# The experts' group of 64 + 32 + 32 slots as four column tiles of 32, and third behind the first group

## The chip, the cores and the metric

One core of one Trainium2 chip runs the whole program. The metric is the device time of one execution in microseconds (us). Engines are named as in the profile: PE (TensorE matmul), PEld (its weight load), DVE (VectorE), ACT (ScalarE), POOL (GpSimd), SP (SyncE, which here only issues transfers).

## The reference, cut to what matters

The program is one block of a hybrid model on 256 tokens of width 1024: four mixers, a merge, and then a mixture of 16 experts, all in float32. Only the experts' part is touched:

```
def _hier_moe(h, w_grp, b_grp, w_rt, b_rt, w1, w3, w2):
    ...                                   # group and top 2 experts of each token, combine: 256 x 16
    out = jnp.zeros_like(t)
    for e in range(N_EXPERTS):            # 16 experts, hidden width 512
        y = (jax.nn.silu(t @ w1[e]) * (t @ w3[e])) @ w2[e]
        out = out + combine[:, e:e + 1] * y
    return out.reshape(shp)
```

Each token uses two experts, but every expert has some tokens, so all 16 experts' weights (6.3 MB each) are read.

## The kernel before, in words

**Slots and groups.** Expert 0 has 128 slots of its own. The other 15 experts are ranked on the chip by how many tokens chose them, and a table, `RANK`, gives each rank a group, an offset and a number of slots: three large ranks get 128, 128 and 96, five get 64, seven get 32. A group has 128 slots, one per row of the result, so there are eight groups, which I number 0 to 7 in the order in which they are multiplied:

| Group | before | after | loads (up + down) |
|---|---|---|---|
| 0 | 128 (expert 0) | the same | 8 + 4 |
| 1 | 64 + 64 | the same | 16 + 8 |
| 2 | 128 | the same | 8 + 4 |
| 3 | 128 | **64 + 32 + 32** | 8 + 4, now 24 + 12 |
| 4 | 64 + 64 | **128** | 16 + 8, now 8 + 4 |
| 5 | 64 + 32 + 32 | **64 + 64** | 24 + 12, now 16 + 8 |
| 6 | 32 + 32 + 32 + 32 | the same | 32 + 16 |
| 7 | 96 + 32 | the same | 16 + 10 |

**A group's work.** `gather` fetches the slots' tokens by a matmul with a one-hot matrix (tiles `Dh`, `h2h`, `h2l`), for two groups at once: 1 and 2, 3 and 4, 5 and 6, and 7 alone. `expert_up` multiplies by w1 and w3: eight steps, a step taking one load of 512 KB per expert of the group (two blocks of 128 rows by 512 columns). `hidden` transposes, `expert_down` multiplies by w2 in four steps, and `scatter` adds the rows back to the tokens by a one-hot matmul (tiles `DT`, `yeh`, `yel`). In program order the down part of group g - 1 stands behind the up part of group g.

**Column tiles.** An expert with 32 slots uses 32 of the array's 128 columns, and its result goes to 32 rows of a shared result bank. The helper `subs` says in which pieces an expert's slots are multiplied: before, 96 slots go as three pieces of 32, everything else as one piece. Each float32 matmul of 512 columns stands in the trace as two records (two passes).

**Loads and places.** All weights go through 34 places of 512 KB (tiles wwA, wh, wb, wC, wD, wB and g), handed out in a fixed ring. The first 12 loads (expert 0) come early. The other 180 need the ranking, start at 506.5 us, and all are issued by SP in program order: `wload` (L281 is the line of the helper that records it) takes the next place, and SP waits until the matmuls that last read that place are done. So load n of these 180 can be issued when the place that was released as number n - 22 is free. A step releases its places at its end. The last group's w2 is loaded in narrower cuts, so that the result leaves in pieces.

All instructions carry line L281, that of a recording helper; they are told apart by tiles.

Of the kernel before, what the change touches and what calls it, by code (L numbers as in the profile page):

```python
# [23 lines left out]


NSTAT = 1
RANK = [(1, 0, 128), (2, 0, 128), (6, 0, 96), (0, 0, 64), (0, 64, 64), (3, 0, 64), (3, 64, 64), (4, 0, 64),
        (6, 96, 32), (4, 64, 32), (4, 96, 32), (5, 0, 32), (5, 32, 32), (5, 64, 32), (5, 96, 32)]
NGRP = NSTAT + 1 + max(g for g, _, _ in RANK)
assert len(RANK) == NE - NSTAT  # L30

# [45 lines left out]
def _consts():  # L77
# [14 lines left out]
    def add3(name, a):  # L92
        add(name, a, 2)
# [68 lines left out]
    add3("tie", row(np.where(i4[None, :] < i4[:, None], -1.2e-38, 0.0)))  # L162
    nd = len(RANK)
    add3("rev", row(nd - 1 - np.arange(nd)))
# [3 lines left out]
    add3("scap", row([128] * NSTAT))  # L168
    add3("rbase", row([128 * (NSTAT + g) + o for g, o, n in RANK]))
    add3("rcap", row([n for g, o, n in RANK]))  # L170
    return [np.ascontiguousarray(np.concatenate(o, 1), dtype=np.float32) for o in outs]
# [117 lines left out]
def body(ctx, tc, I, out, dbg=None, upto=None):  # L289
# [55 lines left out]
    def act(o, i, f=AF.Copy, **k):  # L345
        A.activation(out=o, in_=i, func=f, **k)
# [4 lines left out]
    def ts(o, a, s1, s2=None, op0=mul, op1=add, eng=V):  # L351
        if s2 is None:
            eng.tensor_scalar(out=o, in0=a, scalar1=s1, scalar2=None, op0=op0)
        else:
            eng.tensor_scalar(out=o, in0=a, scalar1=s1, scalar2=s2, op0=op0, op1=op1)

    def tt(o, a, b, op=mul, eng=V):
        eng.tensor_tensor(out=o, in0=a, in1=b, op=op)
# [4 lines left out]
    def red(o, i, op=add):  # L363
        return V.tensor_reduce(out=o, in_=i, axis=AX.X, op=op)

    def mmul(o, l, r, start=True, stop=True, shared=False):
        T.matmul(out=o, lhsT=l, rhs=r, start=start, stop=stop, skip_group_check=shared)
# [34 lines left out]
    def tr(o, i):  # L402
        T.transpose(out=o, in_=i, identity=ident[:i.shape[0], :i.shape[0]])
# [505 lines left out]
    for j in range(31):  # L909
        n, w = 31 - j, j + 1  # L910
# [12 lines left out]
    for m in range(32):  # L923
        d, o = m // 16, (m % 16) * 32
# [9 lines left out]
    for m in range(32):  # L934
        d, o = m // 16, (m % 16) * 32
# [20 lines left out]
    for step in range(8):  # L956
# [29 lines left out]
        if step < 7:  # L986
# [5 lines left out]
            for h in range(2):  # L992
                f_ = fch[hv[h], :, :, step:step + 1].to_broadcast([64, 2, 2, 64])
                o = Sn[hv[h], :, :, hv[h]]
# [5 lines left out]
        if step >= 4:  # L1000
            for d, (c8, t_, vs, us, m0, VU) in enumerate(st):
                for i in range(2):
                    o = py[:, i, c8 - 4, :]
# [376 lines left out]
    def sm(name, shape, bufs=1, dt=F32):  # L1380
        return small(name, shape, bufs, p2, dt)
# [32 lines left out]

    nd = len(RANK)
    key = sm("key", [nd])
# [23 lines left out]
    def hb():  # L1440
        return hb_("hb")

    def mb():
        return mb_("mb")
# [86 lines left out]
    def wload(name, e, q):  # L1531

        w = places.pop(0)
        wn[0] += 1
        src = I[name]
        src = src[e] if isinstance(e, int) else src[bass.ds(e, 1)].rearrange("a d n -> (a d) n")
        j = src.shape[0] // 128
        src = src.rearrange("(p j) n -> p j n", j=j)
        jj = j // 4
        if isinstance(q, slice):  # L1540
            ins = SP.dma_start(w[:, :j * (q.stop - q.start)].rearrange("p (j n) -> p j n", j=j), src[:, :, q])
        else:
            ins = SP.dma_start(w.rearrange("p (j n) -> p j n", j=jj), src[:, q * jj:(q + 1) * jj])
        if wn[0] <= MA + 2:
            after(ins, loads[min(wn[0] + 2, len(loads) - 1)])
        return w

    groups = [[(e, 0, 128)] for e in range(NSTAT)] + [[] for _ in range(NGRP - NSTAT)]
# [4 lines left out]
    def eid(e):  # L1553
        if isinstance(e, int):
            return e
        if e not in regs:
            r = e[1]
            regs[e] = nc.values_load(eidi[0:1, r:r + 1], engines=[mybir.EngineType.SP], min_val=0, max_val=NE - 1,
                                     skip_runtime_bounds_check_because="sum over a one-hot of 16 experts")
        return regs[e]  # L1560

    def subs(o, n):
        if n == 96:
            return [(o + k, 32) for k in range(0, 96, 32)]
        return [(o, n)]

    Dw, Dt = (gg[0][:, 0, k * 512:k * 512 + 512].rearrange("p (a s) -> p a s", a=2) for k in range(2))

# [38 lines left out]
    def expert_up(g, between):  # L1607

        k = next(s.index(g) for s in SETS if g in s)
        gs_ = slice(k * 128, k * 128 + 128)  # L1610
        ph = []
        for name in ("w1", "w3"):
            p = hb()
            ph.append(p)
            for q in range(4):
                ws = [wload(name, eid(e), q) for e, _, _ in groups[g]]
                for jj in range(2):
                    j = 2 * q + jj
                    for w, (e, o, n) in zip(ws, groups[g]):
                        for o_, n_ in subs(o, n):  # L1620
                            mmul(p[o_:o_ + n_], gT[:, j, gs_.start + o_:gs_.start + o_ + n_],
                                 w[:, jj * 512:jj * 512 + 512], j == 0, j == 7)
                places.extend(ws)
            if name == "w1":
                between()
        rows = slice(0, max(o + n for _, o, n in groups[g]))
        pd = mb()
        for a in range(2):
            tr(pd[:, a * 128:a * 128 + 128], Dw[:, a, gs_])
        cw_ = sm("cw", [1], 3)  # L1630
        red(cw_, pd[:, :256])
        DT = slots.tile(p2, [P, 256], F32R, "DT", "DT", 3)
        ts(DT, pd[:, :256], 0.0, None, ALU.is_gt)
        a_ = slots.tile(p2, [P, 512], F32, "act", "act", 1)
        act(a_[rows], ph[0][rows], AF.Silu)
        tt(a_[rows], a_[rows], ph[1][rows])
        return a_, rows, cw_, DT
# [10 lines left out]
    def w2s(g):  # L1648
        if g not in down_w:
            down_w[g] = [[wload("w2", eid(e), j) for e, _, _ in groups[g]] for j in range(4)]  # L1650
        return down_w[g]
# [3 lines left out]
    def parts(py, yh, yl, rows, cw_, cs):  # L1655

        t = slots.tile(p2, [P, 512], F32, "sct", "sct", 2)[:, :cs.stop - cs.start]
        tt(t[rows], py[rows], gg[0][rows, 1, cs])
        act(yh[rows, cs], t[rows], AF.Copy, scale=cw_[rows])
        stt(yl[rows, cs], t[rows], cw_[rows], yh[rows, cs].bitcast(F32), mul, sub)  # L1660

    def scatter(yh, yl, rows, DT, cs):

        for a in range(2):
            as_ = slice(a * 128, a * 128 + 128)
            po = mb()[:, :cs.stop - cs.start]
            mmul(po, DT[rows, as_], yh[rows, cs], True, False)
            mmul(po, DT[rows, as_], yl[rows, cs], False, True)
            tt(x2[:, a, cs], po, x2[:, a, cs], add)
# [3 lines left out]
    def expert_down(g, aT, rows, cw_, DT):  # L1673
        yh, yl = (slots.tile(p2, [P, 1024], F32R, n, n, 1) for n in ("yeh", "yel"))
        if g < NGRP - 1:
            py_ = [hb() for _ in range(2)]
            for j in range(4):
                ws = w2s(g)[j]
                for hf in range(2):
                    for w, (e, o, n) in zip(ws, groups[g]):  # L1680
                        for o_, n_ in subs(o, n):
                            mmul(py_[hf][o_:o_ + n_], aT[:, j, o_:o_ + n_], w[:, halves[hf]], j == 0, j == 3)
                places.extend(ws)
            for hf in range(2):
                parts(py_[hf], yh, yl, rows, cw_, halves[hf])
            return yh, yl

        cuts = [0, 256, 512, 768, 896, 1024]
        cols = [slice(a, b) for a, b in zip(cuts, cuts[1:])]
        ws = [[wload("w2", eid(e), cs) for e, _, _ in groups[g]] for cs in cols]  # L1690
        for q in range(len(cols) + 1):
            if q < len(cols):
                py = hb()
                n_c = cols[q].stop - cols[q].start
                for j in range(4):
                    for w, (e, o, n) in zip(ws[q], groups[g]):
                        for o_, n_ in subs(o, n):
                            mmul(py[o_:o_ + n_, :n_c], aT[:, j, o_:o_ + n_], w[:, j * n_c:j * n_c + n_c], j == 0, j == 3)
                places.extend(ws[q])
                parts(py[:, :n_c], yh, yl, rows, cw_, cols[q])  # L1700
            if q:
                cs = cols[q - 1]
                scatter(yh, yl, rows, DT, cs)
                A.dma_start(ov[:, :, cs], x2[:, :, cs])
# [8 lines left out]
    def down(g):  # L1713
        if g >= 0:
            a_, rows, cw_, DT = state[g]["u"]
            state[g]["y"] = expert_down(g, state[g]["aT"], rows, cw_, DT)
# [92 lines left out]
```

## Time and profile before

| | us |
|---|---|
| median of 3 timed runs | 781.92 |
| the three runs | 775.94, 781.92, 784.67 |
| the profiled execution, its own time | 777.15 |
| its span in the trace | 775.4 |

The span is the time from the first to the last recorded instruction; 1.75 us of the execution lie around it. Times in the views count from the span's start. The experts' part is what follows 506 us.

### The profile page before, as it was taken

What the parts mean: (1) busy time and instruction counts of PE and PEld (TensorE: products, weight loads), DVE (VectorE), ACT (ScalarE), POOL (GpSimd) and SP (SyncE); (2) the same over time, 40 slices, a digit from 0 to 9 for tenths busy, and PEclk for the clock granted to TensorE, in tenths of its full rate; (3) what the DMA queues carried; (4) which work ended last, traced back from release to release, by engine and by line L of the source; (5) the groups of instructions that cost most, each with busy time, mean ns of one, the idle gap of its engine ahead of it and who ended that gap; (6) DMA issues with size and microseconds to landing.
All of it is one profiled execution on the core that took longest, in us unless ns stands there. A gap on an engine that the chain in (4) does not pass through costs nothing.

```text
span 775.4 us, 13568 instructions
## 1 busy us (share of the span) xinstructions
PE 716.7 (92%) x5189; PEld 491.1 (63%) x5189; DVE 471.6 (61%) x1002; ACT 277.1 (36%) x524; POOL 83.4 (11%) x85
## 2 busy tenths in 40 slices
PE   2989998998889999999999999889999999999996
PEld 0559986787778676777999997654454451242234
DVE  5586567789994787899996486773241350230214
ACT  4343453344354676743556334511111110010111
POOL 0140011113100110000102280100000000000000
PEclk9999995799987999999999999969999999999999
DMA  8663320123432025567877885089999899879995
GB/s 318 189 251 109 102 89 1 38 86 97 122 97 83 9 76 191 170 196 251 298 280 256 283 299 194 1 302 409 409 409 407 300 398 333 314 288 399 410 390 170
DMA packets 53897, 174.97 MB, mean 226 GB/s; under 512 B 5442, under 2 KB 12482, under 8 KB 53826
## 3 DMA queue, kind: packets, MB, share of 16 engines
q1 hardware_dynamic: 50896, 168.79, 60.4%
q10 hardware_dynamic: 2930, 5.25, 1.9%
q8 instruction: 42, 0.69, 0.4%
q14 instruction: 29, 0.24, 0.1%
HBM read 172.97 MB, written 1.05 MB: 224 GB/s over the span
## 4 chain that ended last, share of the span: by engine, by line
PE 72%; DVE 15%; DMA 5%; ACT 4%; issue 3%; POOL 1%; SPq 0%; DVEq 0%; ACTq 0%; POOLq 0%
PE hb L281 26%; PE pj L281 16%; PE mm L281 14%; PE mo L281 11%; PE mb L281 5%; DVE wlo L281 2%; DMA mw<-in_wb_dram 2%; DVE TT L281 1%; DVE xt L281 1%; DVE acc L281 1%; DMA raw<-in_wb_dram 1%; DMA wwA<-in_w_dram 1%; ACT prob L281 1%; DMA rk<-in_rg_dram 1%; DVE sin L281 1%
## 5 line engine op out<-in xcount | busy, mean ns | idle before, releaser
L281 PE MATMUL pj<-h,whi 128*128 128x256 f32 x1072 | 203.1, 290 | 2.1 <-DVE ylr L281 2.0
L281 PEld LDWEIGHTS pj<-h,whi 128*128 128x128 f32 x1072 | 169.1, 193 | 12.3 <-issue 7.0
L281 PE MATMUL pj<-h,wlo 128*128 128x256 f32 x536 | 156.0, 292 | 3.5 <-DVE wlo L281 3.4
L281 ACT ACTIVATE whi<-raw 128x512 fp32r<-128x512 f32 x130 | 81.1, 629 | 115.0 <-PE pj L281 88.2
L281 DVE TENSOR_TENSOR wlo<-raw,whi 128x512 fp32r<-128x512 f32 x130 | 92.9, 723 | 27.3 <-ACT whi L281 26.6
L281 PEld LDWEIGHTS pj<-h,wlo 128*128 128x128 f32 x536 | 103.3, 193 | 8.3 <-DVE wlo L281 5.2
L281 DVE TENSOR_TENSOR act<-act,hb 128x512 f32<-128x512 f32 x8 | 5.5, 688 | 90.0 <-PE hb L281 53.4
L281 PE MATMUL hb<-wwA,g 128*32 128x512 f32 (+2 forms) x152 | 44.2, 597 | 0.0
L281 PE MATMUL hb<-wwA,aT 128*64 128x512 f32 (+2 forms) x136 | 39.8, 597 | 0.0
L281 DVE TENSOR_TENSOR sct<-hb,gg 128x512 f32<-128x512 f32 (+2 forms) x19 | 11.3, 606 | 43.4 <-PE hb L281 43.4
L281 ACT ACTIVATE aT<-mb 128x512 f32<-128x512 f32 x8 | 4.8, 598 | 85.7 <-PE hb L281 43.0
L281 ACT ACTIVATE yeh<-sct,cw 128x512 fp32r<-128x512 f32 (+2 forms) x19 | 12.2, 652 | 57.9 <-DVE sct L281 54.5
L281 PE MATMUL hb<-wB,g 128*32 128x512 f32 (+2 forms) x148 | 32.8, 598 | 0.0
L281 ACT ACTIVATE g<-mb,c 128x256 f32<-128x256 f32 (+1 forms) x20 | 9.8, 519 | 51.6 <-PE mb L281 51.6
L281 PE MATMUL hb<-wh,g 128*32 128x512 f32 (+2 forms) x80 | 27.7, 624 | 0.0
L281 PEld LDWEIGHTS hb<-wwA,g 128*32 128x32 f32 (+2 forms) x152 | 12.1, 129 | 23.8 <-issue 22.2
L281 PEld LDWEIGHTS hb<-wwA,aT 128*64 128x64 f32 (+2 forms) x136 | 12.8, 140 | 21.1 <-issue 19.2
L281 DVE TENSOR_TENSOR x<-mb,x 128x512 f32<-128x512 f32 (+2 forms) x38 | 20.9, 599 | 7.4 <-PE mb L281 7.3
L281 DVE SCALAR_TENSOR_TENSOR gg<-adaw,sT,gg 128x512 f32<-128x512 f32 x32 | 23.5, 739 | 1.6 <-ACT gg L281 1.5
L281 PE MATMUL mb<-Dh,h2h 128*128 128x256 f32 (+1 forms) x80 | 20.7, 322 | 4.0 <-DVE Dh L281 3.2
L281 DVE SCALAR_TENSOR_TENSOR acc<-adaw,sT,acc 128x512 f32<-128x512 f32 x32 | 23.8, 772 | 0.0
L281 POOL TENSOR_TENSOR gg<-gg 128x256 f32<-128x256 f32 (+1 forms) x8 | 5.3, 677 | 168.2 <-DVE gg L281 168.2
(479 smaller groups left out, 1409.5 us busy)
## 6 DMA issues: line engine op xcount, KB each, us to landing
wwA<-in_w_dram SPq DMA_DIRECT2D x68, 512.0 KB, 7.7
raw<-in_w_in_dram SPq DMA_DIRECT2D x57, 512.0 KB, 4.0
adaw<-in_ada_dram SPq DMA_DIRECT2D x48, 512.0 KB, 5.0
wB<-in_w_dram SPq DMA_DIRECT2D x38, 512.0 KB, 10.1
wC<-in_w_dram SPq DMA_DIRECT2D x24, 512.0 KB, 8.8
wh<-in_w_dram SPq DMA_DIRECT2D x22, 512.0 KB, 10.1
wD<-in_w_dram SPq DMA_DIRECT2D x18, 512.0 KB, 9.9
wb<-in_w_dram SPq DMA_DIRECT2D x10, 512.0 KB, 10.1
```

Source lines behind the costliest of these rows:

```text
L281: r = f(*a, **k)
```

## The change

`RANK` gives the same slots to the same ranks, but in other groups: the group of 64 + 32 + 32 becomes group 3, and 128 and 64 + 64 come behind it. `subs` now cuts every expert of a group into pieces as large as the group's smallest expert: in the group of 64 + 32 + 32 the expert of 64 becomes two pieces of 32, with the same weights streamed twice. Nothing changes in the other groups (96 + 32 already went as four pieces of 32).

```
-RANK = [(1, 0, 128), (2, 0, 128), (6, 0, 96), (0, 0, 64), (0, 64, 64), (3, 0, 64), (3, 64, 64), (4, 0, 64),
-        (6, 96, 32), (4, 64, 32), (4, 96, 32), (5, 0, 32), (5, 32, 32), (5, 64, 32), (5, 96, 32)]
+RANK = [(1, 0, 128), (3, 0, 128), (6, 0, 96), (0, 0, 64), (0, 64, 64), (4, 0, 64), (4, 64, 64), (2, 0, 64),
+        (6, 96, 32), (2, 64, 32), (2, 96, 32), (5, 0, 32), (5, 32, 32), (5, 64, 32), (5, 96, 32)]
...
-    def subs(o, n):
-        if n == 96:
-            return [(o + k, 32) for k in range(0, 96, 32)]
-        return [(o, n)]
+    def subs(g, o, n):
+
+        m = min(n_ for _, _, n_ in groups[g])
+        return [(o + k, m) for k in range(0, n, m)]
...
-                        for o_, n_ in subs(o, n):
+                        for o_, n_ in subs(g, o, n):
```

(The table counts a rank's group from 0 behind expert 0's, so its group 2 is my group 3; the last edit stands at three places, one in `expert_up` and two in `expert_down`.)

What this does to the order of the instructions, at the places that matter. First PE at the start of group 3's up part, behind group 1's down part (`hb<-wwA,aT`); a row is one matmul or several of one kind, with the slots and columns. Before, group 3 is one expert of 128, a load at a time:

```order
L281 MATMUL hb<-wwA,aT 64x512 x16
L281 MATMUL hb<-wC_5634,g_5633 128x512 x2
L281 MATMUL hb<-wC_5635,g_5633 128x512 x2
L281 MATMUL hb<-wC_5636,g_5633 128x512 x2
L281 MATMUL hb<-wC_5637,g_5633 128x512 x2
L281 MATMUL mb<-ident,act 128x128 x4
```

Now three loads make a step of eight matmuls of 32 slots, four for each block:

```order
L281 MATMUL hb<-wwA,aT 64x512 x16
L281 MATMUL hb<-wC_5634,g_5633 32x512 x2
L281 MATMUL hb<-wC_5635,g_5633 32x512
L281 MATMUL hb<-wC_5636,g_5633 32x512
L281 MATMUL hb<-wC_5634,g_5633 32x512 x2
L281 MATMUL hb<-wC_5635,g_5633 32x512
L281 MATMUL hb<-wC_5636,g_5633 32x512
```

The same step of the group of 64 + 32 + 32 in its old place (group 5) on PE:

```order
L281 MATMUL hb<-wB_5644,g_5633 64x512
L281 MATMUL hb<-wB_5645,g_5633 32x512
L281 MATMUL hb<-wB_5646,g_5633 32x512
L281 MATMUL hb<-wB_5644,g_5633 64x512
L281 MATMUL hb<-wB_5645,g_5633 32x512
L281 MATMUL hb<-wB_5646,g_5633 32x512
```

So six matmuls of two sizes become eight of one. Then PE at the start of group 6, where the last gather is mixed with the group's first matmuls. Now:

```order
L281 MATMUL hb<-wwA,aT 128x512 x8
L281 MATMUL hb<-wC_5634,g_5633 32x512
L281 MATMUL mb<-ident,act 128x128 x4
L281 MATMUL mb<-ident,gg 128x128 x2
L281 MATMUL mb<-Dh,h2h 128x128
L281 MATMUL mb<-Dh,h2l 128x128
L281 MATMUL hb<-wC_5635,g_5633 32x512
L281 MATMUL mb<-Dh,h2h 128x128
```

Before, group 4's down part (`hb<-wh_5648,aT`, `hb<-wwA,aT`) was mixed with that gather; now it is done ahead of it, and single matmuls of group 6's first step stand among the gather's instead.

## Rows read from the trace of the kernel before

**Rows 1.** The page: span, PE, and bandwidth in 40 slices.

```profile
span 775.4 us, 13568 instructions
PE 716.7 (92%) x5189; PEld 491.1 (63%) x5189; DVE 471.6 (61%) x1002; ACT 277.1 (36%) x524; POOL 83.4 (11%) x85
...
GB/s 318 189 251 109 102 89 1 38 86 97 122 97 83 9 76 191 170 196 251 298 280 256 283 299 194 1 302 409 409 409 407 300 398 333 314 288 399 410 390 170
```

**Rows 2.** Stages: window, length, busy of five engines, clock, DMA share, GB/s.

```profile
506.00:520.00 14.00, 12.25 (x39) 9.21 (x40) 11.61 (x41) 3.10 (x6) 0.00 (x0) 0.53 0.86 320
520.00:600.00 80.00, 80.00 (x292) 38.04 (x291) 21.25 (x45) 10.91 (x19) 2.93 (x4) 1.00 1.03 409
600.00:620.00 20.00, 20.00 (x78) 8.41 (x77) 6.62 (x11) 2.53 (x4) 0.00 (x0) 1.00 0.86 303
620.00:640.00 20.00, 20.00 (x86) 10.18 (x82) 10.61 (x23) 3.53 (x6) 1.47 (x2) 1.00 1.01 397
640.00:660.00 20.00, 20.00 (x64) 3.88 (x64) 0.00 (x0) 1.08 (x2) 0.00 (x0) 1.00 0.93 334
660.00:680.00 20.00, 19.73 (x74) 6.53 (x75) 5.29 (x11) 0.46 (x1) 0.91 (x2) 1.00 0.87 317
680.00:690.00 10.00, 9.46 (x45) 4.57 (x42) 4.16 (x8) 3.08 (x6) 0.00 (x0) 1.00 0.99 395
690.00:700.00 10.00, 10.00 (x80) 3.20 (x83) 2.58 (x4) 0.43 (x1) 0.00 (x0) 1.00 0.54 177
700.00:750.00 50.00, 48.37 (x300) 14.43 (x296) 7.41 (x12) 2.70 (x5) 0.00 (x0) 1.00 1.03 408
750.00:765.00 15.00, 14.20 (x141) 6.67 (x137) 8.34 (x17) 3.06 (x6) 0.00 (x0) 1.00 1.00 303
```

**Rows 3.** What SP's load queue waited for, 580 to 700: sum, times, longest.

```profile
SPq L281 <- PE hb L281: 66.0, 46, 7.7
```

**Rows 4.** The same, 700 to 750.

```profile
SPq L281 <- DMA wwA<-in_w_dram: 9.2, 14, 1.1
SPq L281 <- PE hb L281: 6.1, 7, 2.4
```

**Rows 5.** Timeline of PE: start, length, matmul, records (groups 3, 4, 5, 7).

```profile
585.97 7.13 PE L281 MATMUL hb<-wC,g 128*128 128x512 f32 x16
...
611.06 3.60 PE L281 MATMUL hb<-wwA,g 128*64 128x512 f32 x16
...
645.27 4.04 PE L281 MATMUL hb<-wD,g 128*64 128x512 f32 x12
...
736.02 3.62 PE L281 MATMUL hb<-wwA,g 128*32 128x512 f32 x32
```

**Rows 6.** The chain of waits, pieces in order of time: start, length.

```profile
593.57 6.87 PE hb L281 x16
600.44 1.60 PE mb L281 x8
...
624.08 6.46 PE mb L281 x42
```

**Rows 7.** Timeline of PE where group 6 begins among the last gather.

```profile
675.22 0.75 PE L281 MATMUL mb<-ident,act 128*128 128x128 f32 x4
...
676.40 1.95 PE L281 MATMUL hb<-wh,aT 128*64 128x512 f32 x8
...
685.78 1.05 PE L281 MATMUL hb<-wwA,g 128*32 128x512 f32 x2
...
692.48 1.48 PE L281 MATMUL hb<-wwA,g 128*32 128x512 f32 x9
```

**Rows 8.** Loads issued from 606 to 612: number, size, median us from issue to landing.

```profile
wB<-in_w_dram SPq DMA_DIRECT2D x5, 512.0 KB, 5.2
```

**Rows 9.** Two short stretches, columns as in rows 2.

```profile
500.00:504.00 4.00, 1.65 (x9) 1.48 (x9) 2.82 (x14) 3.78 (x2) 0.00 (x0) 0.77 0.00 0
724.00:728.00 4.00, 2.42 (x11) 1.12 (x12) 2.93 (x5) 1.93 (x3) 0.00 (x0) 1.00 1.03 410
```

More of the change, by code (lines that the diff above doesn't have):

```diff
@@ L1680, in expert_down @@
                     for w, (e, o, n) in zip(ws, groups[g]):
-                        for o_, n_ in subs(o, n):
+                        for o_, n_ in subs(g, o, n):
                             mmul(py_[hf][o_:o_ + n_], aT[:, j, o_:o_ + n_], w[:, halves[hf]], j == 0, j == 3)
@@ L1696, in expert_down @@
                     for w, (e, o, n) in zip(ws[q], groups[g]):
-                        for o_, n_ in subs(o, n):
+                        for o_, n_ in subs(g, o, n):
                             mmul(py[o_:o_ + n_, :n_c], aT[:, j, o_:o_ + n_], w[:, j * n_c:j * n_c + n_c], j == 0, j == 3)
```

## The prediction

> **What bounds the kernel now.** I read the page first, then a table of stages, then the waits of the load queue, then PE's timeline. The page says that PE is busy 92% of the span and that from about 520 us the bandwidth stands at 409 GB/s, with dents between 600 and 700 [rows 1]. The stages put numbers on that: 409 GB/s from 520 to 600 and 408 from 700 to 750, less in every stretch between [rows 2]. So about 409 GB/s is what the transfers give when nothing holds them. A load of 512 KB (0.524 MB) then takes 1.28 us. The queue's waits say what holds them: from 580 to 700 SP waited 66.0 us for PE's `hb` matmuls, that is, for a place that PE had not yet released [rows 3]; from 700 to 750 only 6.1 us, and otherwise for earlier loads [rows 4].
>
> So the experts' part has two bounds in turn. From 580 to about 695 PE is late, places come free late, and the transfers starve. From 700 the transfers run full and PE follows them: PE falls idle from 724 to 728 (2.42 busy of 4.00) under 410 GB/s [rows 9]. The chain of waits names PE almost throughout; it doesn't show this turn, the bandwidth does. Therefore PE time is not the currency here. The currency is **bandwidth not used**: a transfer slot lost at 600 is still lost at the end.
>
> What was lost, from 600 to 700, by the six stages [rows 2]: at 409 GB/s 40.9 MB would have come. There came 0.303 x 20 + 0.397 x 20 + 0.334 x 20 + 0.317 x 20 + 0.395 x 10 + 0.177 x 10 (thousand GB/s times us) = 6.06 + 7.94 + 6.68 + 6.34 + 3.95 + 1.77 = 32.74 MB. The missing 8.16 MB are **20.0 us** at 409 GB/s. This is the most that any change of the group order or of PE's speed can win before the last cuts.
>
> **The change part by part.**
>
> *The four column tiles.* A step of the group of 64 + 32 + 32 (one load for each of three experts, two blocks) was 12 records in 4.04 us [rows 5]; successive ones start 3.97 apart. A pair of 64s runs together: 16 records of 64 in 3.60 us, 0.22 each, against 0.43 for a record of 128 (16 in 7.13) [rows 5]. The 64 beside 32s does not: 12 records are 4 rounds of three, 0.99 a round, about two rounds of 0.43 and something for the change of size. Four pieces of 32 run as one round: 32 records of the group of 96 + 32 in 3.62 us, 0.43 for four [rows 5], and three of those four stream the same weights, which is the case that the split 64 brings. So a step costs 4 x 0.43 = 1.72, not 3.97, and the group's 8 + 4 steps save 12 x 2.25 = 27 us of PE. Of these only the part that turns into bandwidth counts.
>
> *The new place.* The group of three experts brings 36 loads (46 us of transfers) for 12 steps (21 us of PE); a group of 128 brings 12 loads (15.4 us) for the same 21 us. Before, the two light groups 2 and 3 stood together, and there the transfers ran dry. Now the heavy group stands between 128 and 128.
>
> Does every place now come free in time? I number the 180 loads. Up to 600 there came 4.48 + 32.72 = 37.2 MB, 71 loads [rows 2]; unhindered, load n lands at 600 + 1.28 (n - 71). A starved load took 5.2 us from issue to landing [rows 8], so its place must be free 5.2 us earlier. PE, from the unchanged 585.97 [rows 5, 6]:
>
> - Group 3 up: the group of 128 took 600.44 - 585.97 = 14.5 with its transposes, and so do eight steps of 1.72. The scatter behind it takes 2.1 (1.60 and one half more). It is mixed with rounds of this group and splits some; a lone matmul of 32 took about 1.0 where a quarter of a round's two passes is 0.22 [rows 7], so I add 3 for four of them. End 605.6.
> - Group 2 down 6.9 (the 16 records of 593.57 are the same amount), to 612.5; group 4 (128) up 14.5, to 627.0; gather and scatter 6.5 [rows 6], to 633.5.
> - Group 3 down begins; its first step ends at **635.2** and releases places 81 to 83, for loads 103 to 105. Load 103 lands at 641.0 unhindered and wants its place by **635.8**. Just in time.
> - Three more steps and transposes to 641; scatter and group 5 up 16.6, to 657.6; group 4 down 6.9, to 664.5. Group 6's first step is mixed with the last gather: from 675.22 to the step's end at about 693 it took 17.7, of which three pieces of 1.95 were group 4's down part, which now stands ahead [rows 7]; 11.9 are left, less by the scatters that now stand behind, say 9 to 12. So its first step ends at **673.5 to 676.5**, and load 135, whose place that is, wants it by 682.0 - 5.2 = **676.8**. In time again.
> - All other places have 3 us or more to spare: group 3's up releases 67 to 90's places from 587.7, 8 us early; group 4's up 13 us early.
>
> So hardly any stall is left. Since two places are within 1 us and my sums of PE are good to 2 or 3 us, I take 1.5 us as left over, with bounds of 0 and 5.
>
> *Not changed in time.* The number of loads, their order inside a group, the overflow test's capacities (each rank keeps its slots) and the queues: no transfer is added, SP passes the same 180 issues. Eight matmuls for six cost PE nothing beyond the rounds counted. After load 172, the last of full width, come group 7's cuts and the tail; they hang on the last loads before and after (303 GB/s from 750 to 765 [rows 2]) and I leave them as they are.
>
> **Sum.** 777.15 (the profiled execution) - 20.0 + 1.5 = **758.7**. Of the four executions known (775.94, 777.15, 781.92, 784.67) the middle is 779.5, 2.4 above the profiled one; half of that added gives my figure, **760**. The three timed ones have a median 4.8 above the profiled one, so a set of three of the new kernel may lie up to 764 for that alone.
>
> **Rivals.**
>
> *The clock falls.* Once transfers bound everything from 600 on, PE waits more: in group 6's down part a step has 1.72 of work for four loads, 5.1 us. In this trace the granted clock fell to 0.53 in the mean of 506 to 520 after PE had been busy 1.65 of 4 us [rows 2, 9], that is, to the lower level of 1.2 GHz; from 724 to 728, with 2.42 of 4, it stayed at 1.00. If it falls late, four-piece steps of 3.44 still hide under 5.1; the two-load steps of group 7 (2.57 of transfers) don't, 8 x 0.87 = 7 us, of which some slack takes a part, and the finish after the last load grows by about 3. 3 to 10 us back: 762 to 769. The Trainium skill says so too: "TensorE: Matmul & The Clock Gate", section "HAM oscillation — how this bites in real kernels", tells of a kernel whose matmul bursts between waits for loads each start at half clock. The trace agrees for the stretch around 500 and not for 724 to 728.
>
> *The four pieces don't run together.* If the split 64 goes one half after the other and then the two 32s, a round is 3 x 0.43 and a step 5.16. Group 3's first down step then ends 9 x (5.16 - 1.72) = 31 us later (eight up steps and itself), 30.4 beyond what load 103 allows, and the three down steps behind release three loads per 5.16 instead of 3.85, 3.9 more: 34 us lost where 20 were won, **791, slower** than before. It decides from a step of 4.0 us: 9 x (4.0 - 1.72) = 20.5. At today's 3.97 it is 777, no change. Against it stands the row of 96 + 32, three pieces from one load at 0.43 a round. The skill's same page, section "Measured speedup vs the span model", gives three column tiles 2.38 times, not 3; four at that efficiency would be an estimated step of 2.17 and some 3.5 us back, 762. The row of 96 + 32 says full speed instead.
>
> *PE later than I sum.* Split rounds or evictions make PE 5 us later at 635 and 676: 4 us of stall, 763. This lies within my bounds.
>
> That the change doesn't do what it says is excluded by the order of instructions: four matmuls of 32 per block in group 3.
>
> **How the numbers follow.** Forecast, with left-over stalls of 0 to 5: 0.72, 755 to 764. Clock: 0.15, 762 to 769. No overlap gained: 0.06, 777. One half after the other: 0.03, 791. Something not thought of, near no change: 0.04. Within 1% of 781.9 (what a measurement of this kernel can't tell from no change) means 774.1 to 789.7. Faster 0.72 + 0.15 + half of the last and a bit = 0.90, the same 0.07, slower 0.03. The range runs from 758.7 less the left-over and the low run's 1.2, and 2 for the tail, 754, to 770, the clock's end.
>
> **What would show it.** Right: 405 GB/s or more in every stage from 600 to about 725; SP's waits for `hb` matmuls small all the way; eight records of group 3 per 0.86 us; the last full load landing near 730 instead of 750, and the same 25 us from there to the end. Wrong: a dent in the bandwidth near 636 to 645 or 677 to 690 (PE late), rounds of group 3 at 0.99 or 1.3 us (no overlap), or a granted clock of 0.5 anywhere from 650 to 745.

## The result, and the profile after

The changed kernel takes **759.11 us** (median of five runs, 757.02 to 765.41) beside 782.04 of the kernel before on the same chip (775.94 to 784.67): a ratio of **0.9733 [0.967, 0.9797]**. A sixth run of 772.8, at a mean clock of 0.938, counts as slow and is left out, as slow runs are in every ratio below. The forecast was 760, with a range of 754 to 770. The profiled execution of the changed kernel is the one of 763.44, its span 761.7.

From the page of the changed kernel, the lines that answer to [rows 1]:

```profile
span 761.7 us, 13664 instructions
PE 704.2 (92%) x5237; PEld 492.2 (65%) x5237; DVE 471.2 (62%) x1002; ACT 277.2 (36%) x524; POOL 82.9 (11%) x85
...
GB/s 318 190 264 84 96 126 1 1 57 114 109 167 85 1 85 122 154 216 230 232 321 244 259 291 255 138 33 401 409 409 408 409 409 409 409 410 384 409 385 146
```

Its stages, columns as in [rows 2]:

```profile
506.00:520.00 14.00, 9.49 (x38) 8.53 (x38) 13.32 (x54) 4.45 (x8) 0.00 (x0) 0.50 0.58 202
520.00:600.00 80.00, 80.00 (x359) 36.56 (x361) 22.97 (x50) 11.50 (x20) 2.93 (x4) 0.98 1.03 409
600.00:620.00 20.00, 20.00 (x77) 7.20 (x66) 6.99 (x11) 1.44 (x2) 0.00 (x0) 1.00 1.03 408
620.00:640.00 20.00, 20.00 (x96) 11.39 (x98) 7.71 (x19) 3.17 (x6) 1.47 (x2) 1.00 1.03 410
640.00:660.00 20.00, 18.38 (x108) 6.64 (x99) 6.56 (x13) 2.53 (x4) 0.91 (x2) 1.00 1.03 408
660.00:680.00 20.00, 19.56 (x77) 8.34 (x74) 5.05 (x9) 3.41 (x6) 0.00 (x0) 1.00 1.03 410
680.00:690.00 10.00, 10.00 (x52) 4.13 (x54) 3.30 (x6) 0.46 (x1) 0.00 (x0) 1.00 1.01 401
690.00:700.00 10.00, 10.00 (x88) 2.90 (x82) 0.22 (x1) 0.60 (x1) 0.00 (x0) 1.00 1.00 365
700.00:725.00 25.00, 23.48 (x162) 8.09 (x162) 6.50 (x11) 2.53 (x4) 0.00 (x0) 1.00 1.03 411
725.00:750.00 25.00, 24.20 (x195) 9.76 (x189) 8.34 (x15) 2.83 (x5) 0.00 (x0) 1.00 0.99 341
```

The dents of [rows 2] between 600 and 680 (303, 397, 334, 317 GB/s) are gone: 408 to 410. One small dent is left, 401 and 365 from 680 to 700. The granted clock is 1.00 from 600 to the end of the table. What SP's load queue waited for from PE, from 584 to 700, against 66.0 us in [rows 3]:

```profile
SPq L281 <- PE hb L281: 19.7, 23, 4.8
```

Most of these 19.7 us cost nothing, because earlier loads were still on their way: load 103 was issued 3.6 behind load 102 and landed only 1.3 behind it.

On PE the four column tiles run as one round. The timeline of PE in group 3's up part (start, length, matmul, records; four records start about every 0.43), then a whole step of its down part, the start of group 6, and the last step of group 6's down part:

```profile
597.24 0.63 PE L281 MATMUL hb<-wB,g 128*32 128x512 f32 x3
597.26 0.62 PE L281 MATMUL hb<-wwA,g 128*32 128x512 f32 x1
597.70 0.60 PE L281 MATMUL hb<-wB,g 128*32 128x512 f32 x3
...
610.12 3.70 PE L281 MATMUL hb<-wh,aT 128*128 128x512 f32 x8
...
643.90 1.95 PE L281 MATMUL hb<-wB,aT 128*32 128x512 f32 x16
...
671.65 1.05 PE L281 MATMUL hb<-wC,g 128*32 128x512 f32 x2
...
734.60 5.30 PE L281 MATMUL hb<-wC,aT 128*32 128x512 f32 x15
```

**A measure that leaves out what the change does not touch.** I call the time from the first issue of a chosen load to DVE's last addition the *experts' part*. It was 263.00 before (506.54 to 769.54) and is 245.56 after (510.50 to 756.06): 17.4 less. In the packets of the load queue (512 KB counted as one load, so the 182 issues of SP count as 180) the time from load 4's landing to load 172's, the last of full width, fell from 235.76 to 216.88; 168 loads at 1.283 are 215.54. What the loads took beyond 1.283 each I call their stall: 20.2 before, 1.3 now, so 18.9 were won there.

The changed kernel's chosen loads start 4.0 us later, in code that is the same in both. The clock explains most of it, since the later falls of the granted clock, the one at 505 included, come 3.2 to 3.3 later than before. One stretch of 20 us shows where it began, before and then after, columns as in [rows 2]:

```profile
40.00:60.00 20.00, 15.96 (x145) 9.70 (x135) 16.21 (x33) 8.01 (x17) 8.49 (x11) 1.00 0.56 218
```

```profile
40.00:60.00 20.00, 18.37 (x111) 9.69 (x112) 12.03 (x27) 7.13 (x17) 6.88 (x10) 0.66 0.56 211
```

PE ran there partly at 1.2 GHz in the changed kernel's execution, at 2.4 in the other. From 523 to 750 the clock is 1.00 in all thirteen traces, so it does not bear on the parts compared below. The five runs follow their clock: 757.02 at a mean of 0.957, 765.41 at 0.946. **So the profiled pair balances:** 777.15 - 18.9 (loads 4 to 172) + 1.5 (last cuts, below) + 4.0 (later start of the loads, mostly the clock) - 0.3 (end of the program) = 763.44.

### The profile page after: what moved, and what is told of

Read it like the earlier page. It is cut to its first block, busy times and chain, and to the rows that moved or that the text cites. A ratio compares the mean times of both kernels' runs of the same rounds, so it can differ in the third digit from the quotient of the medians.

```text
span 761.7 us, 13664 instructions
## 1 busy us (share of the span) xinstructions
PE 704.2 (92%) x5237; PEld 492.2 (65%) x5237; DVE 471.2 (62%) x1002; ACT 277.2 (36%) x524; POOL 82.9 (11%) x85
## 3 DMA queue, kind: packets, MB, share of 16 engines
HBM read 172.97 MB, written 1.05 MB: 228 GB/s over the span
## 4 chain that ended last, share of the span: by engine, by line
PE 70%; DVE 15%; DMA 5%; ACT 4%; issue 3%; POOL 1%; SPq 0%; DVEq 0%; POOLq 0%; ACTq 0%
PE hb L281 25%; PE pj L281 15%; PE mm L281 15%; PE mo L281 10%; PE mb L281 6%; DVE wlo L281 2%; DMA mw<-in_wb_dram 2%; DVE TT L281 2%; DVE acc L281 1%; DMA wwA<-in_w_dram 1%; DMA raw<-in_wb_dram 1%; ACT prob L281 1%; DVE tq L281 1%; DVE sin L281 1%; DMA rk<-in_rg_dram 1%
## 5 line engine op out<-in xcount | busy, mean ns | idle before, releaser
L281 PEld LDWEIGHTS pj<-h,whi 128*128 128x128 f32 x1072 | 169.1, 193 | 12.2 <-issue 7.0
L281 PE MATMUL hb<-wwA,g 128*32 128x512 f32 (+2 forms) x180 | 48.5, 594 | 0.0
L281 PE MATMUL hb<-wwA,aT 128*128 128x512 f32 (+2 forms) x112 | 32.4, 596 | 0.0
L281 PEld LDWEIGHTS hb<-wwA,g 128*32 128x32 f32 (+2 forms) x180 | 16.5, 137 | 23.8 <-issue 22.0
L281 PE MATMUL hb<-wB,g 128*32 128x512 f32 (+1 forms) x144 | 24.4, 594 | 0.0
L281 PEld LDWEIGHTS hb<-wwA,aT 128*128 128x128 f32 (+2 forms) x112 | 12.0, 148 | 17.5 <-issue 16.4
L281 PEld LDWEIGHTS mb<-Dh,h2h 128*128 128x128 f32 x80 | 15.6, 217 | 10.3 <-issue 7.5
```

Of the source, the lines that this page charges most:

```text
L281: r = f(*a, **k)
```

## The experiments

The theory: the loads set the end of the experts' part, and PE counts only where a place comes free too late. Rivals: the split alone would do it, since it is what saves PE time; the move alone would; or PE is the bound and the bandwidth only mirrors it. Ratios are to the kernel before on the same chip. No kernel was traced twice, so how well the experts' part repeats is not shown.

Taken together, the traces bear the theory out. In eleven of the thirteen kernels (before and after included) the experts' part less the stall of loads 4 to 172 is 242.8 to 244.5, whatever the split, the place or the work on PE. Only two lie above, 258.6 and 249.0: those with matmuls added in group 7's up part and in group 6's down part.

### Split without move, and move without split

```diff
 # split alone: the changed subs, and the table of before
+RANK = [(1, 0, 128), (2, 0, 128), (6, 0, 96), (0, 0, 64), (0, 64, 64), (3, 0, 64), (3, 64, 64), (4, 0, 64),
+        (6, 96, 32), (4, 64, 32), (4, 96, 32), (5, 0, 32), (5, 32, 32), (5, 64, 32), (5, 96, 32)]
 # move alone: the changed table, and the subs of before
+    def subs(o, n):
+        if n == 96:
+            return [(o + k, 32) for k in range(0, 96, 32)]
+        return [(o, n)]
```

> The split alone: the group of 64 + 32 + 32 is multiplied as four column tiles of 32, but stays in its old place as group 5. I measure the experts' part from the first issue of a chosen load to the end of the span: 268.8 us before (506.5 to 775.4), 251.2 after the change (510.5 to 761.7). My theory (bandwidth left unused is what counts): the dents from 600 to 640 lie ahead of group 5 and stay, 5.2 + 0.6 = 5.8 us; those behind go, but for 1 to 2 us. So 256 to 259, a time of 764 to 767. Rival A (the split does all, the place nothing): 251 to 252. Rival B (the place does all): 267 to 269, no change.

> The new place alone: the group of 64 + 32 + 32 is group 3, but its 64 stays one column tile, so a step should cost 3.97 us again instead of 1.72. My theory: group 3's first down step ends 9 x 2.25 = 20 us later than in the changed kernel, where it was just in time for load 103, so about 20 us of bandwidth are lost there: experts' part 268 to 273, a time within 1% of before, perhaps slower. Rival A (split does all): also about 268. Rival B (the place does all): 251 to 254. Rival C (each half gives half of the gain): 258 to 262.

These two expectations, and the first two on added work further down, count to the end of the span (268.8 before, 251.2 after). By that measure the split alone took 256.3, as expected, and the move alone 274.7, beyond the expected 268 to 273. The figures from here on count to the last addition.

Split alone: 767.71 us (4 runs), ratio 0.985 [0.9778, 0.9923]; experts' part 250.84. Move alone: 785.12 (10 runs), ratio **1.0089 [1.0043, 1.0134]**; part 269.07. Both together 245.56. So the split alone wins 12.2, the move alone loses 6.1, and behind the split the move wins another 5.3. With the split alone the stall of the two light groups 2 and 3 stays (loads 73 to 84: 4.8 us, 5.2 before), and most of the later ones go. One stage of this kernel, columns as in [rows 2]:

```profile
600.00:620.00 20.00, 20.00 (x70) 8.54 (x69) 6.62 (x11) 1.44 (x2) 0.00 (x0) 1.00 0.92 323
```

With the move alone a step of the heavy group takes 4 us again. The loads stalled 5.4 us at 85 to 100, behind its up part, 8.5 at 101 to 104, where its first down step gives the place, and 11.5 more behind that. Two stages of this kernel:

```profile
620.00:640.00 20.00, 20.00 (x55) 8.16 (x54) 5.54 (x8) 1.76 (x3) 0.00 (x0) 1.00 0.91 332
640.00:660.00 20.00, 20.00 (x80) 9.41 (x80) 7.83 (x19) 2.86 (x6) 1.46 (x2) 1.00 0.56 197
```

This is the prediction's rival of pieces that don't overlap, at today's 3.97 us, run by itself. It was priced at no change, 777; the measured ratio is 0.9% above 1, its interval clear of 1.

### The heavy group in another place

```diff
 # fourth behind the first (groups 2 and 3: 128 each)
+RANK = [(1, 0, 128), (2, 0, 128), (6, 0, 96), (0, 0, 64), (0, 64, 64), (4, 0, 64), (4, 64, 64), (3, 0, 64),
+        (6, 96, 32), (3, 64, 32), (3, 96, 32), (5, 0, 32), (5, 32, 32), (5, 64, 32), (5, 96, 32)]
 # second behind the first (groups 3 and 4: 128 each)
+RANK = [(2, 0, 128), (3, 0, 128), (6, 0, 96), (0, 0, 64), (0, 64, 64), (4, 0, 64), (4, 64, 64), (1, 0, 64),
+        (6, 96, 32), (1, 64, 32), (1, 96, 32), (5, 0, 32), (5, 32, 32), (5, 64, 32), (5, 96, 32)]
```

> Split as in the change, but the group of 64 + 32 + 32 is group 4, behind both groups of 128, with 64 + 64 as group 5. Measured from the first issue of a chosen load to DVE's last addition (263.0 us before, 245.6 after the change, 250.8 for the split alone). My theory: groups 2 and 3 are again 128 and 128, so the dent around loads 73 to 84 comes back, 5 us, and nothing else: 250 to 252. Rival (the split pays, whatever the place): 245 to 247.

> Split as in the change, but the group of 64 + 32 + 32 is group 2, ahead of both groups of 128. Same measure. My theory: by the place-by-place sum no place comes late here, so even the left-over 1.3 us of the changed kernel go, unless the heavy group comes so early that PE waits for its loads: 243.5 to 246, a time of 757 to 760. Rival (two light groups of 128 side by side always starve the transfers): 249 to 252.

Fourth: 762.19 (one run), part 249.66, a hair below the expected range; the loads stalled at 73 to 80, 5.5 us, as with the split alone. Second: 763.07 (4 runs), ratio 0.9797 [0.9741, 0.9852], part 250.92. That is a miss: no stall at 73 to 84, as expected, but 7.6 us at loads 133 to 144. PE came late to group 6. From the first group's down part to group 6's first matmul it took 123.0 (548.14 to 671.16), in the changed kernel 116.6 (555.07 to 671.65). The timeline of PE with the heavy group second, a piece of its up part:

```profile
571.37 1.02 PE L281 MATMUL hb<-wD,g 128*32 128x512 f32 x2
572.32 0.39 PE L281 MATMUL mb<-Dh,h2l 128*128 128x256 f32 x1
...
573.23 1.05 PE L281 MATMUL hb<-wD,g 128*32 128x512 f32 x4
574.21 0.38 PE L281 MATMUL mb<-Dh,h2l 128*128 128x256 f32 x1
...
575.24 1.05 PE L281 MATMUL hb<-wD,g 128*32 128x512 f32 x2
```

The big gather (`Dh`, `h2h`, `h2l`) is mixed into the rounds of four, and a round that is cut costs 1.05 for one or two of its matmuls. Up part, gather, scatter and transposes took 25.9 (555.10 to 580.99), where whole rounds would need 13.8 + 6.4 + 1.2 = 21.4. In the changed kernel the same gather falls behind a group of 128, which has no rounds. So the place also decides which other work cuts the rounds, and this my table of places had left out.

### PE made later, at three places

```diff
 # a helper, called ahead of group 3's down part (first kernel) or group 6's (second): 36 unused matmuls
+    def extra(n, w):
+        pe_ = mb()
+        for _ in range(n):
+            mmul(pe_, w, h2h[:, 0, 0:4].rearrange("p j c -> p (j c)"))
...
+            if g == 3:
+                extra(36, DT[:, :128])
 # third kernel: in group 6's down part, behind steps 2 and 3
+                if g == 6 and j in (1, 2):
+                    pe_ = mb()
+                    for _ in range(3):
+                        mmul(pe_, aT[:, j], ws[3][:, halves[1]])
```

> The changed kernel with 36 extra matmuls of 128 x 512 (0.235 us each by the scatter's rows, 8.5 us together; their result is not used) on PE just ahead of group 3's down part, where I found the places to be released just in time. My theory: load 103 and all behind it come 8 us later, experts' part 258 to 261. If PE has slack there after all: 251 to 254.

> The changed kernel with the same 36 extra matmuls (8.5 us, unused result) on PE in group 7's up part, where PE only follows the loads. They also split rounds of four there, so PE gets 12 to 20 us of work more. My theory (the loads bound this stage, PE time is worth nothing): experts' part 251 to 254. If PE time counts everywhere: 260 or more.

> The changed kernel with six extra matmuls of 128 x 512 (0.86 us each, 5.2 us together, result unused) on PE in group 6's down part, three behind its second and three behind its third step, where PE waits 3.4 us for each next step's loads. The run with 19 us of work in group 7's up part showed 14 us of loss where I expected 0 to 3: either PE time counts there (then this run loses 5, 250 to 251), or only the slack was smaller than the work (then 245.5 to 247).

At group 3 the added work came in one piece, by the timeline of PE in that kernel:

```profile
630.55 8.57 PE L281 MATMUL mb<-h2h,DT 128*128 128x512 f32 x36
```

Time 766.55 (one run), part 253.61, 8.05 more than the changed kernel for 8.57 of work (to the end of the span 261.7, just above the expected 258 to 261). The loads behind it stalled 6.9 us at 101 to 108 and 3.4 at 137 to 144. So the place of load 103 comes just in time: of the 8.57, at most some 1.7 were slack.

At group 6 the time was 774.98 (one run) and the part 259.71, 14.2 more, against 0 to 3 expected (to the end of the span 267.8, against 251 to 254). The work was spread through group 7's up part, mostly three matmuls at a time, and broke its rounds:

```profile
719.12 1.06 PE L281 MATMUL hb<-wB,g 128*32 128x512 f32 x6
720.11 0.97 PE L281 MATMUL mb<-h2h,DT 128*128 128x512 f32 x3
721.01 1.91 PE L281 MATMUL hb<-wB,g 128*32 128x512 f32 x10
```

PE came 17.6 us late to group 6's down part (739.09 - 505.39 against 726.61 - 510.50), within the 12 to 20 that the expectation had counted on, and some 3.4 of that vanished. So the schedule did what was foreseen, and the theory missed: PE time is free in this stage only up to a slack of about 3.4 us; beyond that PE sets the end. The loads landed as early as in the changed kernel (the last one 240.3 behind the first issue, against 240.0).

The third took 758.7 (one run), part 249.93, 4.4 more for 5.5 of work, which seemed to say that PE counts one to one there. Its timeline says otherwise. The schedule had moved group 7's transposes between the matmuls of the last step:

```profile
728.55 1.91 PE L281 MATMUL hb<-wC,aT 128*32 128x512 f32 x8
730.39 0.62 PE L281 MATMUL mb<-ident,act 128*128 128x128 f32 x3
730.95 1.90 PE L281 MATMUL hb<-wC,aT 128*32 128x512 f32 x4
732.78 0.39 PE L281 MATMUL mb<-ident,act 128*128 128x128 f32 x1
733.10 1.90 PE L281 MATMUL hb<-wC,aT 128*32 128x512 f32 x4
```

Eight records, two experts, take 1.91, and so do four of one expert. Without the transposes between them the last two experts run together too, at the latest in a second 1.9, and beside the first two at best; the step ends at 730.5 to 732.4, not at 735.0. By this estimate 2.6 us or more of the 4.4 are the moved transposes; that was not run by itself, and this run doesn't decide on PE's slack; the next two do.

### PE made earlier, and later without moving a round

```diff
 # less PE work: groups 4 and 5 are not scattered
-        if g >= 0:
+        if g >= 0 and g not in (4, 5):
...
 # more PE work, in group 5's down part
+                if g == 5 and j == 2:
+                    pe_ = mb()
+                    for _ in range(4):
+                        mmul(pe_, aT[:, j], ws[1][:, halves[1]])
```

> The changed kernel without the scatter of groups 4 and 5 (their rows are not added to the tokens): PE loses 8 matmuls within group 6's first steps (3.3 us, 683.84 to 687.14) and, ahead of group 7's up part, 8 more with the wait for ACT's yeh and the rounds they break (1.5 + 3.3 + 1.4 us): 9.5 us less of PE in all, no load changed. Theory, that the loads set the end and PE only touches them at group 3's down part, at group 6's second step and in the last few us: the stalls of 1.3 at group 6's second step go and little else, experts' part 243.5 to 244.5 (245.56 before the cut), with group 6's last down step, 5.3 in the row of 15 records, still following its four loads 1.28 apart, and the steps ahead of it stretched in the same way. Rival, that PE is the bound behind group 6's first step: 236 to 238.

> The changed kernel with four unused float32 matmuls of full width (3.7 us by the row of 0.9 each in the experiment before with 6 in 2.76 for three) in group 5's down part, behind its third step; the schedule also puts group 6's transposes and the scatter a little later, among group 7's first rounds, which breaks some. All matmuls of group 6's down part keep their order, so that PE comes 4 to 6 us late to group 7 and no round of the last step is split, unlike in the experiment with work behind group 6's down steps. Theory (PE is some 4 us ahead of the loads at the end): experts' part 245.5 to 247.5. Rival (PE counts one to one there): 249 to 252.

Less work: 759.28 (2 runs), ratio 0.977 [0.9657, 0.9882]; part **244.72**, 0.84 less, 0.2 above the expected range. The 9.5 us were a sum made beforehand; in the trace PE came 6.4 earlier to group 6's down part (718.43 - 508.77 = 209.66 against 216.11). More work: 760.41 (2 runs), ratio 0.9784 [0.9656, 0.9912]; part **245.55**, the same to 0.01, though PE came 3.0 us later to group 6's down part (729.31 - 510.18 = 219.13 against 216.11). The rival that PE is the bound is out: 6.4 earlier wins 0.8, 3.0 later costs nothing.

Where did the 6.4 go? Into waits for loads that the timeline counts as busy. PE in the kernel with less work, 28 of the 32 records of group 6's second and third down steps, then the last step:

```profile
722.58 9.15 PE L281 MATMUL hb<-wwA,aT 128*32 128x512 f32 x28
...
732.01 5.31 PE L281 MATMUL hb<-wC,aT 128*32 128x512 f32 x15
```

Sixteen such records take 1.95 when their loads are there (643.90 above); here 28 take 9.15, and a new expert's records start every 1.28. One expert's load lands every 1.28 us, and each expert's four records start about 2.65 behind its load (in the changed kernel 734.14, 735.42, 736.69, 738.00 for landings at 731.51, 732.78, 734.07, 735.34). No idle time shows, since one expert's records, 1.9 one behind the other, outlast the 1.28. So 15 records in 5.30 is the sign of a wait for loads.

### The gather earlier, and wider last cuts

```diff
 # the gather of group 7 ahead of group 6's up part
-            if g + 1 == s[0]:
+            if g + (2 if n == 4 else 1) == s[0]:
                 gather(n)
 # wider last cuts
-        cuts = [0, 256, 512, 768, 896, 1024]
+        cuts = [0, 256, 512, 768, 1024]
```

> The changed kernel with the gather for group 7 placed ahead of group 6's up part instead of behind it, so that it is mixed into group 3's last down steps and group 5's up part, not into the four-piece rounds of group 6. In the changed kernel these rounds were broken: six single matmuls of 32 slots took 1.05 each (1.04 to 1.05, about 671 to 686), where their share of a whole round's two records is 0.22, so 4 to 5 us of PE are lost there, and SP waited 1.3 us in all for places that group 6's second step releases. If PE and the transfers are tied (my reading), the stall of 1.3 goes and some of PE's time behind it comes back at the end: experts' part 241.5 to 244.5 instead of 245.56. If the places of group 3's down part and of group 5, which now wait behind some 5 us more of gather and scatter, have no slack (load 103's place came 0.2 us before it was wanted), the loads stall there instead: 246 to 250. If the breaks only move to group 3's and 5's rounds: 245 to 246.

> The changed kernel with the last group's w2 in four cuts of 256 columns instead of three of 256 and two of 128. The last eight loads took 14.6 us in the changed kernel against 10.3 for full rows; four loads of the 256 cut took 5.9. So the last loads should land 2.8 us earlier, and the work behind the last load grow by 1.7 to 2.8 us (matmuls, eviction and addition of 256 columns instead of 128, and the output transfer). Same measure, to the last addition: 243 to 246. If the cuts don't matter to the transfers: 247 to 248.

The gather earlier: 759.92 (4 runs), ratio 0.9753 [0.9692, 0.9814]; part 245.36, the third of the three outcomes. Group 6's rounds are cut at two places in place of six, but those of group 3's last steps and the pairs of group 5 are cut instead, and the loads stalled 1.6 us at 133 to 136 in place of 1.3 at 137 to 144. Wider cuts: 765.48 (4 runs), ratio 0.9849 [0.9784, 0.9914]; part 245.35, no gain where 0 to 2.5 us were expected, and to the end of the span 1.1 more (252.3). Rows of 1 KB landed no faster than those of 512 bytes: the last 1 MB took 5.9 us here and 5.6 in the changed kernel. The loads of 1 KB rows ahead of it took 1.5 per 512 KB in both, against 1.28 for full rows. No version that does all the work beat the changed kernel by more than 0.2 us in this part.

**The last cuts.** From load 172 to the last one it took 13.67 before and 15.16 after. The 1.5 lies in the last 512 KB. Share of the DMA engines from 3 to 1 us ahead of the last landing, before and then after, columns as in [rows 2]:

```profile
760.90:762.90 2.00, 2.00 (x24) 1.15 (x27) 1.49 (x4) 0.51 (x1) 0.00 (x0) 1.00 0.98 243
```

```profile
747.50:749.50 2.00, 2.00 (x24) 1.12 (x27) 1.41 (x4) 0.51 (x1) 0.00 (x0) 1.00 0.38 103
```

In the changed kernel a few packets are left over while most engines have none: on average 1.4 packets of the load queue are in flight from 2 to 1 us ahead of the last landing and 1.2 in the last us (12.5 and 3.3 before), against 17.5 while the loads run full. The last landing is 239.7 to 240.3 after the first issue in all six kernels whose stalls sum to 1.3 or less, whether load 172 came early or late (less work: 1.3 earlier at load 172, 0.3 earlier at the end). With the gather earlier, which stalled 2.0, it is 239.3, earlier still. This fits a few engines that fall behind while the loads run full and catch up when they stall. The trace does not name a packet's engine, and why some are behind was not tested.

## Why the prediction was right, step by step

- **The bandwidth as currency, 20.0 us to win.** Right: 18.9 won between loads 4 and 172. PE 6.4 earlier and 3.0 later at group 6's down part moved the end by 0.8 and 0.0. But PE was only about 3.4 us ahead of the loads at the end, so PE time is free there only up to that. One ground was misread, too: PE's idle time from 724 to 728 was not a wait for loads. It ended with ACT's `yeh`, and the changed kernel has the same wait. SP's waits alone carried the argument. The better sign in PE's rows was group 6's last down steps. PE's row behind that wait, before and then after, with the idle time in brackets:

```profile
725.58 0.73 PE L281 MATMUL mb<-yeh,DT 128*128 128x512 f32 x2 [1.63 <-ACT yeh L281]
```

```profile
709.31 0.73 PE L281 MATMUL mb<-yeh,DT 128*128 128x512 f32 x2 [1.52 <-ACT yeh L281]
```

- **A step of 1.72.** Right: four records per 0.43, 16 in 1.95 with the first one's start. The Trainium skill, "TensorE: Matmul & The Clock Gate", section "Measured speedup vs the span model", has three column tiles at 2.38 times. The trace shows more for four: they run in the 0.43 that one record of 128 slots takes, with one weight shared by two of them.
- **Group 3's up part, 19.6, and its first down step at 635.2.** It took 20.56 (589.56 to 610.12), and the step ended at 639.4, 635.4 less the later start of 4.0. Right to 1 us.
- **Load 103 just in time.** Right: no stall there, and 8.57 of added work cost 8.05. It had at most some 1.7 to spare, where the prediction had 0.6.
- **Group 6's first step at 673.5 to 676.5.** SP issued into its places from 679.9, 675.9 less the 4.0. In time, as forecast.
- **"All other places have 3 us or more to spare."** Wrong for group 6's second step, which I had not worked out: its places for loads 139 to 142 came late (SP issued at 688.56, 684.6 less the 4.0, wanted by about 682), because gather and scatter cut its rounds too, 1.05 each. It cost 1.3 us. So the 1.5 left over were met in size, but at another place than the two I named, which is luck.
- **The tail unchanged.** Wrong by 1.5, in the last 512 KB: the experts' part won 17.4 of the 18.9.
- **760.** The sum against the profiled execution was 758.7; that execution of the changed kernel took 763.44, of which 4.0 are the later start of the loads and 1.5 the last cuts. The medians differ by more than the profiled pair (22.9 against 13.7), and by 5.5 more than the 17.4 of the experts' part. No trace of a median run is kept, so where those 5.5 lie stays open; the clock ahead of the experts is likely, but not shown. That 760 met the median to 1 us is luck in that part.
- **The clock.** It stayed at 1.00 from 522 to 757, so the rival is out. PE had 23.48 busy of 25 in the stage that I feared, 700 to 725, though the timeline counts some waits as busy. What the Trainium skill tells under "HAM oscillation — how this bites in real kernels" ("TensorE: Matmul & The Clock Gate") did not come here, though the loads set the pace. The stretch around 500, which the prediction put beside it, was no such case: nothing was loading there (0 GB/s in [rows 9]).
- **The rival on the other side**, no overlap: excluded by the rounds. Its condition, a step near 4 us in the new place, was run as the move alone and came out slower by 0.9%, where I had put the turning point at exactly no change. The experts' part was 6.1 longer than before. The rival put its whole loss of some 20 us at load 103. By the packets load 104 landed only 14.3 later than in the changed kernel, 5.4 of them stalls at loads 85 to 100, where with steps of 4 us the up part of group 3 gives its places late too. The other 10 or so were lost behind load 104, mostly at 113 to 120 and 133 to 144, where the rival had nothing.

## What to carry to other kernels

Where a ring of places feeds one engine, sum the bandwidth that is not used, and ask of each place when it is released and when it is wanted; the difference says what a faster step is worth, and where it is worth nothing. Order heavy and light groups so that their loads and their work balance over the length of the ring, but only after the step of the heavy one is cheap: the same move lost 6 us with the old step and won 5 with the new one. Where PE follows the loads, ask by how much: beyond that slack, here some 3 us, PE sets the end after all. Before adding or moving work beside column tiles, look at where the schedule will put it: a single 128-wide matmul inside a round costs more than its own time.

## What the runs showed of the hardware

- A round of four column tiles of 32 (float32, 512 columns) takes 0.43 for four records, whichever of them share a weight. A lone matmul of 32 (two records) in a cut round takes 1.05. Two matmuls on the same column tile run one behind the other: their four records take 1.9.
- Code that is the same in all kernels, ahead of the experts, ended between 501.2 and 510.6 us in thirteen traces, and the times of the changed kernel's five runs follow their granted clock. The experts' part, not the total, was used to tell variants apart; whether it repeats to 1 us was not measured.
- With loads running full for 240 us, the mean share of the 16 DMA engines fell to 0.38 from 3 to 1 us ahead of the last landing (0.98 before, where the loads had stalled).
